# Attention: the weave of the log-sum-exps, the place of the forget-gate rows, of the factors and of four copies

## The chip, the cores and the metric

The kernel runs on one core of one Trainium2 chip. The metric is the device time of one execution in microseconds (us). A core has a matrix engine (TensorE, PE in the profile, its weight loads PEld), VectorE (DVE), ScalarE (ACT), GpSimd (POOL) and SyncE (SP); SP issues nearly all DMAs here, one after the other. Each engine works through its own queue in order.

## The reference

A decoder trunk of two layers over 528 tokens (16 learned ones ahead of 512), width 1024: forgetting attention, a gated MLP with a short convolution, a gated linear recurrence, and another such MLP. All is float32. The change lies in the attention of layer 0, with 16 heads of 64:

```python
xn = rms_norm(h, norm_g)
q, k, v, f_logit, o_gate = jnp.split(xn @ w_in, [D, 2 * D, 3 * D, 3 * D + H], axis=-1)
q = rms_norm(q.reshape(B, L, H, hd), q_gain).astype(jnp.float32) * (hd ** -0.5)
k = rms_norm(k.reshape(B, L, H, hd), k_gain).astype(jnp.float32)
log_f = jax.nn.log_sigmoid((f_logit + b_f).astype(jnp.float32))
c = jnp.cumsum(log_f, axis=1).transpose(0, 2, 1)
...
s = jnp.einsum('bqhd,bkhd->bhqk', q_blk, k)
s = s + c_blk[..., None] - c[:, :, None, :]
s = jnp.where(q_pos[:, None] >= key_pos[None, :], s, -jnp.inf)
p = jax.nn.softmax(s, axis=-1)
...
o = o * jax.nn.sigmoid(o_gate)
return o @ w_out
```

## The kernel before

Activations lie with features on the partitions and the 528 tokens along the free axis. A float32 matrix product is made of three matmuls on split operands: each operand is a rounded part `hi` (float32r) and a remainder `lo`, and hi·hi, lo·hi and hi·lo are accumulated (L263, L266, L267 in `proj_unit`; L312 in `values`). `weights` loads a weight tile to `raw` (L207, issued by SP, two buffers), casts it to `hi` on ScalarE (L210) and subtracts to get `lo` on VectorE (L126, the line of the helper `sub`).

The attention (`fox`) takes its 16 heads as eight pairs. A loop over p from -3 to 7 makes one step of the pipeline. In each step generators are woven by `weave`: every part has a number, and at each turn the part whose yielded sum over that number is smallest is advanced to its next yield. Thus a number larger than the sum of the part's yields makes it end before the step does. The parts of step p are:

- the fill: the projections of query and key of pair p+3 (`stage_a`), of values for two pairs at a time (`stage_v`, by `values`), of the output gate (`stage_g`, from step 4), and in the last step half of the output projection for four blocks (`stage_p`);
- `stage_n(p + 2)`: the factors of the query and key norm. `stage_a` ends with sums of squares (`strow`, L548), which go by four small DMAs to `am` (L553), through a reciprocal root on VectorE, and by two DMAs to `rows` (L563). `stage_n` spreads them by a matmul (L577, PSUM bank d, one buffer), multiplies query and key by them on VectorE (L578), splits into hi and lo (`stg`), and calls `pack`;
- `pack`: six DMAs (L604) that put the split query and key of two heads into two of six slots `pk` (`k1`, `q1`, `k2`, `q2`);
- `stage_l(p + 1)`: first four small DMAs (L613) that put the cumulated forget gates `cneg` into two rows of each head's `k1`, then `lse` for each of the two heads: scores by block of queries (L735, L736, the mask L738, PSUM bank s with four buffers), the row maximum on VectorE (L748, L754, L755), the sum of exponentials on ScalarE (L119), the logarithm, a transpose by matmul of `lr` (L770), and three DMAs of `lrow` into two rows of `q1` (L775, L776). Its yields add up to 2.0 a head;
- `stage_t(p)`: after a yield of 2.75 the attention proper (`attend`): scores with the log-sum-exp already in the operands (L792, L793), masked on VectorE (L796), the exponential on ScalarE (`pt`), times values (L807, PSUM bank c).

Values come in blocks of 128 tokens and one of 16 (the "lone" ones). The 16 are computed in another way (L295, L302), and `put` copies each block from PSUM (bank p, two buffers) to `v`, times the token's norm factor: L593, on ScalarE.

The program's order gives each instruction its priority; at build time a scheduler with a model of durations puts them into the queue of each engine, so that an instruction may be placed ahead of an earlier one that is not ready yet by that model. On the chip the queues run in the order so fixed.

Of the kernel before, what the change touches and what calls it, by code (L numbers as in the profile page):

```python
# [16 lines left out]
AF = mybir.ActivationFunctionType  # L17
ALU = mybir.AluOpType
# [9 lines left out]
NPAIR = 8  # L28
# [28 lines left out]
def weave(*parts):  # L57

    live = [[g, 0.0, cost] for g, cost in parts if g is not None]
    while live:  # L60
        x = min(live, key=lambda r: r[1] / r[2])
        try:
            x[1] += next(x[0])
        except StopIteration:
            live.remove(x)


def take(gen, share):

    for cost in gen:  # L70
        yield cost
        share -= cost
        if share <= 0:
            return
# [8 lines left out]
class Builder:  # L83
# [297 lines left out]
    def fox(self, ctx):  # L381
        nc, tc, a = self.nc, self.tc, self.a
# [53 lines left out]
        for g in range(4):  # L436
            t0, tn = full[g % 2]
# [10 lines left out]
        def stage_f():  # L448

            zr = s2.tile([HF, T], F32, name="zr", tag="strow", bufs=1)  # L450
            for t0, tn in full:
                psf = self.bank("c")
                o = psf[:HF, :tn]
                for k in range(KT):
                    xh, xl = self.xhi[:, k, t0 : t0 + tn], self.xlo[:, k, t0 : t0 + tn]
                    mm(psf[:, :tn], wfs[k][:, 0:P], xh, start=k == 0, stop=False)
                    mm(psf[:, :tn], wfs[k][:, 32 : 32 + P], xl, start=False, stop=k == KT - 1)
                    if k % 2:
                        yield 0.44
                zv = zr[:, t0 : t0 + tn]  # L460
                nc.scalar.copy(zv, psf[32 : 32 + HF, :tn])
                nc.vector.tensor_tensor(zv, o, zv, ALU.add)
                nc.vector.tensor_tensor(zv, zv, self.rsb[:HF, t0 : t0 + tn], ALU.mult)
            nc.sync.dma_start(z, zr.rearrange("h (j c) -> h j c", c=CW))
# [28 lines left out]
        def stage_g(ms, outs):  # L493

            for m, out in zip(ms, outs):
                wt = self.weights(a["wg"][m], KT)
                for t0, tn in full:
                    ps = bank()
                    yield from self.proj_unit(ps[:, :tn], [wt], self.x, t0, tn)
                    nc.vector.tensor_tensor(out[:, t0 : t0 + tn], ps[:, :tn], self.rsb[:, t0 : t0 + tn], ALU.mult)  # L500


                e = self.sqp.tile([P, T], F32, name="e", tag="sq")
                nc.vector.tensor_scalar(out, out, -87.0, None, ALU.max)
                self.act(e, out, AF.Exp, scale=-1.0)
                self.act(out, e, AF.Ln, bias=ones1)
                self.act(out, out, AF.Exp, scale=-1.0)
                nc.vector.scalar_tensor_tensor(e, e, 1.0, out, ALU.add, ALU.mult)
                nc.vector.scalar_tensor_tensor(out, e, 2.0, out, ALU.subtract, ALU.mult)
# [58 lines left out]

        def stage_n(p):

            raw, rows = scaled.pop(p)
            stg = s2.tile([P, 4, T], F32R, name="stg", tag="stg", bufs=1)
            for w_, nm in ((0, "q"), (1, "k")):
                hh, ll = stg[:, 2 - 2 * w_, :], stg[:, 3 - 2 * w_, :]
                for i, (t0, tn) in enumerate(full):
                    bc = self.bank("d")
                    mm(bc[:, :tn], selr[:, 2 * w_ + i, :], rows, start=True, stop=True)  # L577
                    nc.vector.tensor_tensor(  # L578
                        raw[nm][:, t0 : t0 + tn], raw[nm][:, t0 : t0 + tn], bc[:, :tn], ALU.mult
                    )  # L580
                    yield 0.11
                nc.scalar.copy(hh, raw[nm])
                self.sub(ll, raw[nm], hh.bitcast(F32))
            pack(p, stg)

        def stage_v(p):

            v = vs[(p // 2) % NV]

            def put(t, o):  # L590
                tn = o.shape[0]
                r = rs[:tn, rcol[t] : rcol[t] + 1]
                nc.scalar.activation(v[:tn, t, :, :], o.rearrange("p (b c) -> p b c", c=64), AF.Copy, scale=r)  # L593

            yield from self.values(a["wv"][p // 2], KTL, put, lone, 16, "ppppp")

        def pack(p, stg):
            packs[p] = []
            for hd in range(2):
                head = 2 * p + hd  # L600
                d = slots[head % NSLOT]
                packs[p].append(d)
                sl = slice(64 * hd, 64 * hd + 64)
                dma = lambda o, i: nc.sync.dma_start(o.bitcast(F32), i.bitcast(F32))  # L604
                dma(d["pk"][0:64, 0:2, :], stg[sl, 0:3:2, :])
                dma(d["pk"][0:64, 2:4, :], stg[sl, 0:4:3, :])
                dma(d["pk"][64:128, 2:4, :], stg[sl, 1:3, :])

        def stage_l(p):
            for hd, d in enumerate(packs[p]):  # L610
                head = 2 * p + hd
                for x in range(2):
                    nc.sync.dma_start(  # L613
                        d["k1"][64 + x : 65 + x, :].rearrange("x (j c) -> x j c", c=CW).bitcast(F32),
                        cneg[8 * head : 8 * head + 8, x, :].bitcast(F32),
                    )
            for d in packs[p]:
                yield from self.lse(d, s2, identb, maskq)

        def stage_t(p):  # L620

            yield 2.75
            for o0, o1 in ((0, 256), (256, 528)):
                po = self.bank("c")
                yield from self.attend(o0, o1, p, packs[p], vs[(p // 2) % NV], po, s2, maskk)
                nc.vector.tensor_copy(gate[:, p, o0:o1], po[:, : o1 - o0])
# [38 lines left out]
        def stage_p():  # L665

            for m in range(NEARLY):
                nc.sync.dma_start(self.h[:, m, :], a["h0"][:, m, :])
                yield from out_proj(m, 0, 4, hold=True)
# [6 lines left out]
        for p in range(-3, NPAIR):  # L676
            fill, cost = [], 0.0
            if p % 2 and 0 <= p + 1 < NPAIR:
                fill.append(vgen[p + 1])
                cost += half if p > 0 else 2 * half  # L680
            if p + 3 < NPAIR:
                fill.append(stage_a(p + 3))
                cost += 12.8
            if p % 2 == 0 and 0 <= p < NPAIR - 2:
                fill.append(take(vgen[p + 2], half))
                cost += half
            if p in gplan:
                fill.append(stage_g(gplan[p], [late[m % 4] for m in gplan[p]]))
                cost += 5.4 * len(gplan[p])
            if p == NPAIR - 1:  # L690
                fill.append(stage_p())
                cost += 2.7 * NEARLY
            weave(
                (chain(*fill), 0.97 * cost),
                (stage_n(p + 2) if 0 <= p + 2 < NPAIR else None, 1.0),
                (stage_l(p + 1) if 0 <= p + 1 < NPAIR else None, 4.3),
                (stage_t(p) if p >= 0 else None, 8.5),
                (stage_f() if p == -2 else None, 3.5),
            )
            if p == -2:  # L700
                forget()
            gated += gplan.get(p, ())
            while gated and p >= max(gated[0], 5 + gated[0] // 4):
                m = gated.pop(0)
                o = gate[:, m, :]
                nc.vector.scalar_tensor_tensor(o, o, -1.0, late[m % 4], ALU.mult, ALU.mult)
                ohi, olo = (slots[s]["pk"][:, m % 4, :] for s in ((4, 5) if m < 4 else (0, 1)))
                nc.scalar.copy(ohi, o)
                self.sub(olo, o, ohi.bitcast(F32))
                ox.append((ohi, olo))  # L710
# [832 lines left out]
```

## Time and profile before

| | us |
|---|---|
| median of 3 runs | 1457.14 |
| lowest and highest of them | 1457.02, 1458.89 |
| the profiled execution | 1460.8 |
| its span, first to last instruction | 1458.7 |

Mean granted TensorE clock over the span: 0.994. In the profile a line such as `L793 MATMUL pss<-pk` names the line of the kernel, the operation, and the tiles written and read; `pss` is PSUM bank s. A bracket at the end of a timeline row is the engine's idle time before the instruction and what ended it. Matmuls overlap: where they follow each other without a stop, the distance of their starts, and not the duration, tells their pace. Queue rows of SP are the time that issuing took, not the transfer. Times in the trace count from the first instruction. The attention lies between the start and about 370 us; step -1 begins near 45 us, the pair-by-pair attention (`stage_t`) runs from 100 to 355 us.

### The profile page before, as it was taken

The numbers are of one execution on the slowest core, as the hardware profiler recorded it, in microseconds if no ns is written. First come the engines' busy times: TensorE is split into PE (matmuls) and PEld (weight loads), VectorE is DVE, ScalarE is ACT, GpSimd is POOL, SyncE is SP. The second block draws the span as 40 slices with busy tenths as digits, with TensorE's granted clock in tenths as the row PEclk, the third lists the DMA queues.
The fourth block names the chain that finished last, engine by engine and source line by source line (L and its number), as shares of the span: only waits on it lengthen the run. The fifth ranks groups of instructions, "written<-read, shape, count | busy, mean of one in ns | idle before, by whom it ended". The sixth has DMA issues, their size and how long they took to land.

```text
span 1458.7 us, 29188 instructions
## 1 busy us (share of the span) xinstructions
PE 1431.1 (98%) x11482; PEld 1351.5 (93%) x11482; DVE 973.4 (67%) x2080; ACT 664.6 (46%) x1293; POOL 151.5 (10%) x271
## 2 busy tenths in 40 slices
PE   7999999998999999999999999999999999999998
PEld 6888888888999999999998999999999999999997
DVE  7555555774667665666785676677667877866773
ACT  5355555573434444333563223332445565544551
POOL 7000000001112100111001101011011110000000
PEclk9999999999999999999999999999999999999999
DMA  4443344435999884678737527284587795544542
GB/s 160 119 106 90 90 107 125 134 82 128 299 231 242 214 253 138 171 193 199 217 93 181 147 43 178 68 188 110 124 235 162 213 280 166 174 141 138 162 145 88
DMA packets 99697, 230.98 MB, mean 158 GB/s; under 512 B 13528, under 2 KB 15320, under 8 KB 99560
## 3 DMA queue, kind: packets, MB, share of 16 engines
q1 hardware_dynamic: 79400, 188.47, 40.5%
q0 software_dynamic: 20160, 40.64, 18.3%
q8 instruction: 90, 1.47, 0.4%
q14 instruction: 47, 0.39, 0.1%
HBM read 213.62 MB, written 75.24 MB: 198 GB/s over the span
## 4 chain that ended last, share of the span: by engine, by line
PE 90%; DMA 4%; DVE 2%; ACT 2%; issue 1%; SPq 1%; ACTq 0%; DVEq 0%
PE psp L263 8%; PE psp L267 8%; PE psp L266 8%; PE pss L263 8%; PE pss L267 8%; PE pss L266 8%; PE psp L312 6%; PE psp L1300 2%; PE psp L1301 2%; PE psp L1302 2%; PE psc L807 2%; PE pss L961 1%; PE psp L1194 1%; PE psp L1195 1%; PE psp L1196 1%; PE psd L1302 1%
## 5 line engine op out<-in xcount | busy, mean ns | idle before, releaser
L210 ACT CAST hi<-raw 128x1024 fp32r<-128x1024 f32 (+3 forms) x250 | 234.2, 940 | 365.4 <-PE psp L266 88.7
L126 DVE TENSOR_TENSOR lo<-raw,hi 128x1024 fp32r<-128x1024 f32 (+3 forms) x254 | 275.5, 1088 | 98.4 <-ACT hi L210 94.6
L263 PE MATMUL psp<-xhi,hi 128*128 128x264 f32 (+1 forms) x984 | 283.2, 289 | 6.3 <-ACT xhi L332 6.3
L266 PE MATMUL psp<-xlo,hi 128*128 128x264 f32 (+1 forms) x984 | 283.4, 288 | 2.6 <-DVE xlo L333 2.6
L267 PE MATMUL psp<-xhi,lo 128*128 128x264 f32 (+1 forms) x984 | 284.3, 289 | 0.0
L263 PEld LDWEIGHTS psp<-xhi,hi 128*128 128x128 f32 x984 | 186.6, 190 | 9.6 <-ACT xhi L332 6.3
L266 PEld LDWEIGHTS psp<-xlo,hi 128*128 128x128 f32 x984 | 187.1, 190 | 4.9 <-DVE xlo L333 3.5
L267 PEld LDWEIGHTS psp<-xhi,lo 128*128 128x128 f32 x984 | 187.1, 190 | 1.5 <-issue 1.5
L267 PE MATMUL pss<-xhi,lo 128*128 128x264 f32 (+3 forms) x520 | 149.9, 288 | 0.0
L263 PE MATMUL pss<-xhi,hi 128*128 128x264 f32 (+3 forms) x520 | 149.3, 288 | 0.1
L266 PE MATMUL pss<-xlo,hi 128*128 128x264 f32 (+3 forms) x520 | 149.2, 287 | 0.0
L232 POOL DMA_DIRECT2D s<-gu x80 | 66.2, 846 | 332.6 <-DMA s<-gu 297.0
L263 PEld LDWEIGHTS pss<-xhi,hi 128*128 128x128 f32 x520 | 97.8, 188 | 0.9 <-ACT xhi L332 0.3
L267 PEld LDWEIGHTS pss<-xhi,lo 128*128 128x128 f32 x520 | 97.7, 188 | 0.7
L266 PEld LDWEIGHTS pss<-xlo,hi 128*128 128x128 f32 x520 | 97.8, 188 | 0.7
L312 PE MATMUL psp<-hi,xhi 128*128 128x256 f32 x232 | 67.6, 291 | 3.0 <-ACT v L593 3.0
L267 PE MATMUL pss<-room,lo 128*128 128x512 f32 (+1 forms) x182 | 70.3, 386 | 0.0
L266 PE MATMUL pss<-room,hi 128*128 128x512 f32 (+1 forms) x182 | 70.2, 386 | 0.0
L263 PE MATMUL pss<-room,hi 128*128 128x512 f32 (+1 forms) x182 | 69.4, 386 | 0.6 <-ACT hi L210 0.6
L1167 ACT CAST hi<-left 128x768 fp32r<-128x768 f32 (+1 forms) x56 | 43.3, 781 | 54.2 <-PE psp L1195 18.0
L1302 PE MATMUL psp<-xhi,lo 128*128 128x258 f32 x240 | 67.7, 282 | 0.0
L1300 PE MATMUL psp<-xhi,hi 128*128 128x258 f32 x240 | 67.7, 282 | 0.0
(488 smaller groups left out, 3811.3 us busy)
## 6 DMA issues: line engine op xcount, KB each, us to landing
raw<-gu SPq DMA_DIRECT2D x48, 512.0 KB
s<-gu SPq DMA_DIRECT2D x80, 256.0 KB
s<-gu POOLq DMA_DIRECT2D x80, 256.0 KB, 5.7
raw<-gu SPq DMA_DIRECT2D x60, 256.0 KB
pk<-stg SPq DMA_DIRECT2D x48, 264.0 KB
raw<-s SPq DMA_DIRECT2D x40, 256.0 KB
raw<-s SPq DMA_DIRECT2D x20, 512.0 KB
raw<-wqk SPq DMA_DIRECT2D x14, 512.0 KB
```

What stands on the lines that cost most here:

```text
L126: self.nc.vector.tensor_tensor(out, x, y, ALU.subtract)
L210: nc.scalar.copy(hi, raw)
L232: nc.gpsimd.dma_start(out, y, accum_op=ALU.add, max_dma_last_dim=4 * n)
L263: ins = mm(ps, hi[:, i, :], xh, start=k == 0, stop=False)
L266: mm(ps, hi[:, i, :], xl, start=False, stop=False)
L267: mm(ps, lo[:, i, :], xh, start=False, stop=k == total - 1)
L312: mm(ps[:tn, :256], y[:, t0 : t0 + tn], w, start=n == 0, stop=n == 23)
L807: ins = mm(o, v[:, j, 2 * (p % 2) + hd, :], w[hd][0], start=j == 0, stop=j == last)
L1167: nc.scalar.copy(hi, raw)
L1300: mm(ps, hi[:, k0 + k, :], xh, start=start and k == 0, stop=False, skip_group_check=not start)
L1301: mm(ps, hi[:, k0 + k, :], xl, start=False, stop=False, skip_group_check=not start)
L1302: mm(ps, lo[:, k0 + k, :], xh, start=False, stop=k == 3, skip_group_check=not start)
```

## The change

Four edits, all in `fox`:

1. `stage_l` is woven with 5.7 instead of 4.3, `stage_n` with 1.3 instead of 1.0.
2. `stage_n` begins with a yield of 0.45, so that its first matmul comes later in the step.
3. The four DMAs of the forget-gate rows are taken out of `stage_l` into `decays`, which for the pairs 1 to 7 is called right behind `pack`; for pair 0, where the gates are not there yet at that time, it stays at the start of `stage_l`.
4. The copy of the 16 lone values in `stage_v` is done by VectorE; the blocks of 128 stay on ScalarE.

```diff
         def stage_n(p):
 
+            yield 0.45
             raw, rows = scaled.pop(p)
...
             def put(t, o):
                 tn = o.shape[0]
                 r = rs[:tn, rcol[t] : rcol[t] + 1]
-                nc.scalar.activation(v[:tn, t, :, :], o.rearrange("p (b c) -> p b c", c=64), AF.Copy, scale=r)
+                o = o.rearrange("p (b c) -> p b c", c=64)
+                if tn == 16:
+                    nc.vector.tensor_scalar(v[:tn, t, :, :], o, r, None, ALU.mult)
+                else:
+                    nc.scalar.activation(v[:tn, t, :, :], o, AF.Copy, scale=r)
...
                 dma(d["pk"][64:128, 2:4, :], stg[sl, 1:3, :])
-
-        def stage_l(p):
+            if p:
+                decays(p)
+
+        def decays(p):
+
             for hd, d in enumerate(packs[p]):
                 head = 2 * p + hd
                 for x in range(2):
...
+        def stage_l(p):
+            if p == 0:
+                decays(0)
             for d in packs[p]:
                 yield from self.lse(d, s2, identb, maskq)
...
-                (stage_n(p + 2) if 0 <= p + 2 < NPAIR else None, 1.0),
-                (stage_l(p + 1) if 0 <= p + 1 < NPAIR else None, 4.3),
+                (stage_n(p + 2) if 0 <= p + 2 < NPAIR else None, 1.3),
+                (stage_l(p + 1) if 0 <= p + 1 < NPAIR else None, 5.7),
```

## The prediction, made before the result was known

> **What bounds the kernel now.** I read the page first, then the waits of TensorE alone within the attention stage (the first 420 us), then the timelines round each of its long waits.
>
> ```profile
> span 1458.7 us, 29188 instructions
> PE 1431.1 (98%) x11482; PEld 1351.5 (93%) x11482; DVE 973.4 (67%) x2080; ACT 664.6 (46%) x1293; POOL 151.5 (10%) x271
> PE 90%; DMA 4%; DVE 2%; ACT 2%; issue 1%; SPq 1%; ACTq 0%; DVEq 0%
> ```
>
> The reader is to see that TensorE (PE) is the bound: busy 98% of the span, and 90% of the chain that ended last. The change removes no matmul and adds none. It can win only where PE stands still or runs at a lower clock, and lose only by making it stand still in new places. So the question is which of PE's waits in the attention stage the edits reach. The waits of PE, columns total, times, longest:
>
> ```profile
> PE psp L263 <- ACT xhi L332: 6.3, 1, 6.3
> PE pss L792 <- DMA pk<-lrow: 4.0, 1, 4.0
> PE psp L312 <- ACT v L593: 3.0, 3, 1.7
> PE pss L735 <- DMA pk<-cneg: 1.0, 1, 1.0
> PE psd L577 <- DMA rows<-yr: 1.0, 1, 1.0
> PE pss L770 <- DVE lr L126: 0.8, 1, 0.8
> ```
>
> The first is the start of the kernel, which the diff leaves alone. The other five add up to 9.8 us and are, line by line, what the diff touches: the log-sum-exp rows (lrow, lr), the values (v), the forget-gate rows (cneg) and the factors (rows). A wait of PE also costs clock, which the windows show (PE busy and instructions, then the same of the other engines, PEclk, DMA):
>
> ```profile
> 50.00:57.00 7.00, 5.35 (x32) 5.21 (x32) 3.97 (x10) 2.79 (x6) 0.00 (x0) 0.76 0.27 86
> 305.00:333.00 28.00, 26.62 (x203) 23.19 (x202) 19.58 (x58) 17.74 (x54) 0.95 (x1) 1.00 0.27 69
> 337.00:343.00 6.00, 5.73 (x27) 5.74 (x28) 2.02 (x5) 1.56 (x4) 1.46 (x2) 0.52 0.46 68
> 343.00:355.00 12.00, 12.00 (x100) 10.13 (x98) 4.76 (x13) 5.25 (x13) 0.98 (x2) 1.00 0.74 176
> ```
>
> The granted clock is 0.52 in the 6 us behind the wait for lrow and 1.00 again from 343 us.
>
> **Part 1: log-sum-exps at 5.7 instead of 4.3 (stage_l).** The weave takes, at each turn, the part with the smallest share done, share being the sum of its yields over its number. One pair's stage_l yields 2 x (4 x 0.3 + 0.6 + 0.2) = 4.0. It ended at 4.0/4.3 = 0.93 of a step and now ends at 4.0/5.7 = 0.70. In the steps p = 0 to 5 nothing waits for its end, as stage_t of that pair starts only 2.75/8.5 = 0.32 into the next step. The last step is different, because few projections are left to run in front of stage_t(7). PE's timeline and the queue of SP there:
>
> ```profile
> 332.72 0.22 PE L770 MATMUL pss<-identr,lr 128*128 128x128 f32 x1
> 332.95 0.28 PE L793 MATMUL pss<-pk 128*128 128x256 f32 x1
> 337.27 0.58 PE L792 MATMUL pss<-pk 98*128 98x256 f32 x1 [4.03 <-DMA pk<-lrow]
> 338.08 0.42 PE L266 MATMUL psp<-pk,hi 128*128 128x264 f32 x1
> 338.30 0.42 PE L267 MATMUL psp<-pk,lo 128*128 128x264 f32 x1
> 343.34 0.28 PE L266 MATMUL psp<-pk,hi 128*128 128x264 f32 x1
> 343.46 0.28 PE L267 MATMUL psp<-pk,lo 128*128 128x264 f32 x1
> 333.60 1.26 SPq L775 DMA_DIRECT2D pk<-lrow  x2
> 334.90 0.61 SPq L776 DMA_DIRECT2D pk<-lrow  x1
> ```
>
> The transpose of the last log-sum-exps (L770) runs at 332.72, its row is sent until 334.90 + 0.61 = 335.51, and it is there at 337.27, 1.8 us on. PE had asked at 333.2 and sat 4.03 us. Step p = 6 lasts about 28 us (305 to 333). Ending 0.93 - 0.70 = 0.23 of it earlier moves L770 by 6.4 us, and the landing to 337.3 - 6.4 = 330.9, ahead of 332.95. So the 4.03 us go. With them goes the slow clock: from 337.3 to 342.7 the matmuls start 0.22 us apart (338.08, 338.30), later 0.12 (343.34, 343.46), so 5.4 us of work would have taken 5.4 x 0.52 = 2.8 us, and 2.6 us are won. Sum of part 1: **-6.6 us**. Late next is VectorE: the same step already shows PE held 0.8 us by lr, and the max, subtract and exp work of two heads now stands closer together. I take 0 for that wait; its bounds are -0.8 (gone) and +1.6 (once per head).
>
> [...]
>
> **Part 2: the factors later (stage_n).** Four broadcasts stood at 0, 0.11, 0.22 and 0.33 of a step and the packing at 0.44. They now stand at 0.45/1.3 = 0.35 to 0.60, and the packing at 0.89/1.3 = 0.68. The middle steps take some 34 us (130 to 164), so the first moves by 12 us, the packing by 8.2.
>
> ```profile
> 139.51 0.28 PE L266 MATMUL psp<-xlo,hi 128*128 128x264 f32 x1
> 140.77 0.36 PE L577 MATMUL psd<-rows,selr 128*128 128x264 f32 x1 [0.97 <-DMA rows<-yr]
> 57.69 6.14 SPq L604 DMA_DIRECT2D pk<-stg  x6
> 193.58 2.82 SPq L613 DMA_DIRECT2D pk<-cneg  x4
> 73.02 0.25 PE L735 MATMUL pss<-pk 66*128 66x16 f32 x1 [1.03 <-DMA pk<-cneg]
> ```
>
> The wait for rows at 139.51 is covered by the 12 us: **-1.0 us**. What the delay uses up is the time between packing and the next step's log-sum-exps, now 0.32 x 34 = 10.9 us.
>
> **Part 3: the forget-gate rows with the packing (decays).** No DMA is added; for pairs 1 to 7 the four of L613 go from the start of stage_l to behind the six of L604. SP then issues 6.14 + 2.82 = 9.0 us on end, and the last lands 1.8 us later (as lrow did): 10.8 us, against 10.9 available. Before, they were issued in the step itself and landed 2.8 + 1.8 = 4.6 us into it. So the log-sum-exps can begin up to 4.7 us sooner, and that is also what a late packing may lose before they are worse off. The rows wait for cneg (done before step p = -1) and for the slot's last reader, stage_t of three pairs before: both done. Behind the ten stand the square sums (am), the factors (rows) and weight loads; two weight buffers cover them. Pair 0 keeps its place, so the 1.03 us at 73.02 stays. Value: **+1.0 us**, one further wait of that kind; bounds 0 and, at seven of them, +7.
>
> **Part 4: the lone values by VectorE (put).** Four instructions (the groups by shape of ScalarE; the source view of L299 for the nearest of VectorE):
>
> ```profile
> L593 ACT ACTIVATE v<-psp,rst 16x256 f32<-16x256 f32 x4 | 1.8, 456 | 0.9 <-PE psc L807 0.9
> L299 DVE COPY part<-psp x4: 405/408/424, 46.6 to 226.1; 128x256 f32<-128x256 f32 x4
> ```
>
> By VectorE each should take 408 to 456 ns, 1.7 us in all on an engine that is 67% busy: nothing by itself, and at most 1.7 if no gap took it. What counts is where they queue:
>
> ```profile
> 100.98 0.28 PE L312 MATMUL psp<-hi,xlo 128*128 128x256 f32 x1
> 102.42 0.39 PE L312 MATMUL psp<-hi,xhi 128*128 128x256 f32 x1 [1.17 <-ACT v L593]
> 100.96 1.05 ACT L210 CAST hi<-raw 128x1024 fp32r<-128x1024 f32 x1 [1.30 <-DMA raw<-wqk]
> 101.91 0.46 ACT L593 ACTIVATE v<-psp,rst 16x256 f32<-16x256 f32 x1
> 98.46 0.19 DVE L556 TENSOR_TENSOR am<-am,et 64x33 f32<-64x33 f32 x1 [2.21 <-DMA am<-strow]
> 102.04 1.23 DVE L126 TENSOR_TENSOR lo<-raw,hi 128x1024 fp32r<-128x1024 f32 x1 [0.70 <-ACT hi L210]
> 49.66 1.05 ACT L210 CAST hi<-raw 128x1024 fp32r<-128x1024 f32 x1 [3.94 <-DMA raw<-wqk]
> 51.26 0.82 ACT L593 ACTIVATE v<-psp,rst 128x256 f32<-128x256 f32 x2
> 51.79 0.39 PE L312 MATMUL psp<-hi,xhi 128*128 128x256 f32 x1 [1.65 <-ACT v L593]
> ```
>
> At 100.98 PE waits for the PSUM bank of the lone value, whose copy stands on ScalarE behind a weight cast that itself waits for a load. VectorE is at work on other things from 98.46 and idle 0.70 us before 102.04, so it would free the bank earlier: **-1.2 us**. At 51.79 it is different: of the two copies the one of the ordinary block comes first (51.26), PE starts again 0.53 us after that, and that copy stays on ScalarE behind the same cast. So those 1.65 us and the 1.7 of clock I leave in: 0, with -3.4 as the bound.
>
> **Sum.** -6.6 - 1.0 + 1.0 - 1.2 = -7.8 us. Against the profiled execution (1460.8 us, of which 1458.7 are the span) this gives 1453.0; the median of the runs shown is 1457.1, 3.7 us less, and from it the forecast is 1457.1 - 7.8 = **1449.3**. The stage after it is PE-bound too (PE busy 12.00 of 12 from 343), so that what is won at 337 us should last to the end.
>
> **Rivals.**
> 1. *The last row comes as late as before.* The lr of L770 could be set by VectorE and ScalarE, not by the weave; the 0.8 us at lr speaks for it, PE busy 26.62 of 28 with VectorE only 19.58 of 28 speaks against. Then -1.0 + 1.0 - 1.2 = -1.2: 1455.9.
> 2. *Slower: the weights behind the packing.* Ten DMAs are sent in one block, and the packing waits for stg with all loads behind it on SP. If a weight cast then comes late, PE stops as at 51.79: 1.65 + 1.7 = 3.4 us a time. For it speaks that both waits for v go back to a cast that waited for raw<-wqk (3.94 and 1.30 idle); against, that no projection waits for a cast anywhere in the list of PE's waits. It decides from 3 of the six steps on (10.2 against the 8.8 gained); at four, 13.6 - 8.8 = +4.8: 1461.9.
> 3. *More goes.* With the VectorE copy the values' banks change hands otherwise and the 3.4 us at 50 us go as well, and the 0.8 at lr: -12.0, 1445.1.
>
> **How the numbers follow.** Forecast 0.53, with a range of its own of 1446 to 1454 (parts 1 and 4 at their bounds); rival 1 0.20; rival 2 0.17; rival 3 0.10. A measurement of this kernel tells about 0.2% (2.9 us) from no change. The forecast and rival 3 are faster by more, with a little of rival 1: 0.64; the rest of rival 1 is the same, 0.19; rival 2 slower, 0.17. The range from 1444 to 1461 holds everything but the far half of rival 2 and the tails.
>
> **What would show it.** Part 1: no wait for lrow at L792 and a clock of 1.00 through the last step. Part 2: no wait at L577. Part 3: L613 behind L604 on SP; at most one wait at L735. Part 4: no wait for v at the second group of values, the first unchanged. Wrong would be: a wait of PE over 1.5 us within steps 0 to 5 with a clock under 1.00, above all L263 or L312 for hi or lo.

## The result and the profile after

The change makes the kernel slower: 1471.78 us (median; 1466.72 to 1475.41) against 1458.02 (1456.31 to 1460.94) for the kernel before on the same chip, a ratio of 1.0087 with an interval of 1.0061 to 1.0113. The forecast was 1449.3 in a range of 1444 to 1461: wrong in sign. The profiled execution of the changed kernel took 1466.76 us and is among its shortest, so the trace shows less of the loss than the median does.

The page of the changed kernel, the same three lines as before (the transpose L770 is now L782, the scores L792 are L804, the log-sum-exp scores L735 are L747):

```profile
span 1464.7 us, 29178 instructions
PE 1430.6 (98%) x11482; PEld 1351.1 (92%) x11482; DVE 975.6 (67%) x2084; ACT 662.0 (45%) x1289; POOL 152.0 (10%) x271
PE 90%; DMA 4%; DVE 2%; ACT 2%; issue 1%; SPq 0%; ACTq 0%; DVEq 0%
```

The same matmuls, the same bound, and PE busy for 0.5 us less than before (1431.1) in a span 6.0 us longer: the time went into waits. Up to the end of the last product with the values PE runs 2607 matmuls in both kernels. It ends them at 355.1 us before, having been busy for 335.75 us, and at 365.0 us after, busy for 336.52: it stood still for 9.1 us more. PE's waits in the first 420 us (total, times, longest):

```profile
PE pss L782 <- DVE lr L126: 6.5, 2, 5.5
PE psp L263 <- ACT xhi L332: 6.2, 1, 6.2
PE psp L312 <- ACT v L598: 4.6, 3, 2.2
...
PE pss L747 <- ACT pt L119: 2.2, 1, 2.2
PE psp L263 <- ACT rawq L540: 1.6, 1, 1.6
PE pss L804 <- DVE lrow L784: 1.4, 1, 1.4
PE psd L578 <- DMA rows<-yr: 1.2, 2, 0.7
```

The wait for the DMA of lrow (4.0) and the one for cneg (1.0) are gone. In their place the wait for lr has grown from 0.8 to 6.5 us, and three are new: for pt, for rawq and for lrow on VectorE. Where the work was lost is told by windows, first of the kernel before, then of the changed one (stretch, length, busy time and count of PE, PEld, DVE, ACT and POOL, granted clock, DMA share, GB/s):

```profile
100.00:164.00 64.00, 61.86 (x494) 53.51 (x493) 34.87 (x119) 34.90 (x109) 0.90 (x8) 1.00 0.36 94
222.00:240.00 18.00, 17.78 (x139) 14.25 (x139) 9.52 (x37) 7.34 (x24) 0.23 (x2) 1.00 0.38 109
307.00:370.00 63.00, 57.59 (x433) 52.05 (x432) 37.55 (x97) 31.77 (x82) 5.82 (x7) 0.95 0.51 126
```

```profile
100.00:164.00 64.00, 59.29 (x470) 50.86 (x469) 35.57 (x120) 35.93 (x108) 0.67 (x6) 1.00 0.43 118
222.00:240.00 18.00, 14.43 (x60) 9.93 (x59) 8.34 (x33) 7.53 (x25) 0.20 (x2) 0.62 0.27 90
307.00:370.00 63.00, 56.28 (x417) 48.56 (x417) 35.36 (x99) 31.40 (x91) 4.46 (x7) 0.92 0.42 107
```

The matmuls (the count behind PE's busy time) fall short in three places: by 24, by 79 and by 16. In the 18 us from 222 both the waits and the clock of 0.62 are new. What follows the last product with the values takes 1104 and 1100 us, and 1100 to 1108 in every other profile of this study, in no order that goes with the edits. So the loss arises in the attention.

The end of step p = 6, where before all was quiet, on PE and then on SP:

```profile
324.64 0.23 PE L750 MATMUL pss<-maskq,identb 128*128 128x128 bf16 x1
330.36 0.45 PE L782 MATMUL pss<-identr,lr 128*128 128x128 f32 x1 [5.49 <-DVE lr L126]
330.60 0.54 PE L804 MATMUL pss<-pk 98*128 98x256 f32 x1
```

```profile
316.66 0.63 SPq L788 DMA_DIRECT2D pk<-lrow  x1
```

PE stands 5.49 us at the transpose of the last pair's first head. Behind it in its queue stands a score of pair 6 (L804), whose log-sum-exp row had been sent by 317.3 us. In the queue that score is held back by the transpose ahead of it. How the transpose came to stand there is the question of the experiments.

### The profile page after: what moved, and what is told of

Read it like the earlier page. It is cut to its first block, busy times and chain, and to the rows that moved or that the text cites. A ratio compares the mean times of both kernels' runs of the same rounds, so it can differ in the third digit from the quotient of the medians.

```text
span 1464.7 us, 29178 instructions
## 1 busy us (share of the span) xinstructions
PE 1430.6 (98%) x11482; PEld 1351.1 (92%) x11482; DVE 975.6 (67%) x2084; ACT 662.0 (45%) x1289; POOL 152.0 (10%) x271
## 4 chain that ended last, share of the span: by engine, by line
PE 90%; DMA 4%; DVE 2%; ACT 2%; issue 1%; SPq 0%; ACTq 0%; DVEq 0%
PE psp L263 9%; PE psp L267 9%; PE psp L266 9%; PE pss L267 8%; PE pss L266 8%; PE pss L263 8%; PE psp L312 5%; PE psp L1314 2%; PE psp L1312 2%; PE psp L1313 2%; DMA raw<-gu 2%; PE psc L819 2%; PE psp L1206 1%; PE psp L1207 1%; PE psp L1208 1%; PE pss L973 1%
```

## The experiments

All ratios are to the kernel before on the same chip, with 95% intervals.

| run | what it is | ratio | interval |
|---|---|---|---|
| e1_late | only the factors later | 0.9976 | 0.9962 to 0.9990 |
| e2_lse | only 5.7 | 1.0051 | 1.0034 to 1.0069 |
| e3_rows | only the rows with the packing | 0.9998 | 0.9981 to 1.0016 |
| e4_lone | only the lone copies by VectorE | 1.0013 | 0.9998 to 1.0028 |
| e9_lse56 | only 5.6 | 1.0093 | 1.0073 to 1.0112 |
| e10_lse555 | only 5.55 | 1.0006 | 0.9991 to 1.0021 |
| e6_lse55 | only 5.5 | 0.9952 | 0.9937 to 0.9968 |
| e11_lse_t26 | 5.7, first yield of `stage_t` 2.6 | 0.9946 | 0.9932 to 0.9961 |
| e5_lse_t19 | 5.7, first yield of `stage_t` 1.9 | 1.0029 | 1.0009 to 1.0049 |
| e7_after_t19 | whole change, first yield 1.9 | 1.0056 | 1.0039 to 1.0074 |
| e8_no_lse | whole change with 4.3 | 1.0019 | 0.9997 to 1.0041 |
| e12_after55 | whole change with 5.5 | 1.0044 | 1.0027 to 1.0060 |
| e13_late55 | 5.5 and the factors later | 0.9965 | 0.9950 to 0.9979 |
| e14_lone55 | 5.5 and the lone copies | 1.0039 | 1.0018 to 1.0060 |
| e15_no_lone | whole change without the lone copies | 1.0108 | 1.0080 to 1.0136 |
| e16_no_late | whole change without the later factors | 1.0140 | 1.0122 to 1.0159 |
| e17_after_gp | whole change, rows issued by GpSimd | 1.0041 | 1.0021 to 1.0062 |
| e18_lse_rows | 5.7 and the rows with the packing | 1.0074 | 1.0049 to 1.0100 |

**Each edit alone.** Four kernels, each with one part of the diff: the factors, then the number of `stage_l`, the rows, and the lone copies (the last two as in the diff above).

```diff
         def stage_n(p):
+            yield 0.45
...
-                (stage_n(p + 2) if 0 <= p + 2 < NPAIR else None, 1.0),
+                (stage_n(p + 2) if 0 <= p + 2 < NPAIR else None, 1.3),
```

> Only the factors later (the yield of 0.45 and 1.3 instead of 1.0 for stage_n). Theory 1 (queue of SP): the packing, the sums and the loads behind it on SP come later, so weight casts on ScalarE wait for late loads, and PE stops for what stands behind the cast; this edit alone then costs most of the 12 us: ratio 1.005 to 1.010, with the log-sum-exps of the pairs 2 to 7 starting 5 us or more later than before. Theory 2 (proportion): the 5.7 is the cause, and this edit alone gives 0.999 to 1.002. Theory 3 (forget-gate rows behind the packing): also 0.999 to 1.002 here.

```diff
-                (stage_l(p + 1) if 0 <= p + 1 < NPAIR else None, 4.3),
+                (stage_l(p + 1) if 0 <= p + 1 < NPAIR else None, 5.7),
```

> Only 5.7 instead of 4.3 for stage_l. Theory 1: it does no harm by itself; the wait of 4 us for lrow in the last step goes, ratio 0.995 to 0.999. Theory 2: log-sum-exps and scores crowd VectorE and ScalarE, new waits of PE for lr or for the exponentials, ratio 1.005 to 1.010. Theory 3: as theory 1.

```diff
...
+            if p:
+                decays(p)
...
+        def stage_l(p):
+            if p == 0:
+                decays(0)
```

> Only the forget-gate rows sent with the packing. Theories 1 and 2: within 0.2% of before, since SP sent these rows ahead of the packing in the kernel before as well, when their slot came free. Theory 3: ratio 1.004 or more, with a packing or a load that stands behind the rows.

```diff
...
+                if tn == 16:
+                    nc.vector.tensor_scalar(v[:tn, t, :, :], o, r, None, ALU.mult)
...
```

> Only the copy of the lone values by VectorE. All theories: 0.998 to 1.001; the wait of 1.2 us for v at the second group of values is gone or smaller.

The largest single loss is in the edit from which the largest gain was forecast: 5.7 alone costs 0.5%. The factors alone gain 0.24% (some 3.5 us), though the wait for rows that they were to remove is still there (1.2 us in e1_late). The rows alone do nothing. The lone copies alone do nothing that is clear of zero. Of the theories, that of proportion expected the size of the loss of 5.7 (1.005 to 1.010); none expected a gain from the factors.

**Where the weave turns.** The first theory after e2 was a matter of order. A head's `lse` yields 4 x 0.3 + 0.6 = 1.8, then issues its tail with the transpose, and only then the last 0.2. `stage_t` begins, after its yield of 2.75 over a number of 8.5, at a share of 0.3235. With 4.3 the first head has reached 1.8/4.3 = 0.419 before its tail, so scores of the pair at work are issued ahead of the transpose. With 5.7 it is at 1.8/5.7 = 0.316, the smaller share, and the transpose of the next pair's first head is issued ahead of every score. Behind it in PE's queue the scores wait, as L804 did behind the 5.49 us above. The first score of the second pair and that transpose, of the kernel before, the changed one, and e2_lse:

```profile
134.55 0.29 PE L792 MATMUL pss<-pk 98*128 98x256 f32 x1
144.28 0.22 PE L770 MATMUL pss<-identr,lr 128*128 128x128 f32 x1
```

```profile
148.46 0.33 PE L782 MATMUL pss<-identr,lr 128*128 128x128 f32 x1
148.63 0.33 PE L804 MATMUL pss<-pk 98*128 98x256 f32 x1
```

```profile
147.78 0.22 PE L770 MATMUL pss<-identr,lr 128*128 128x128 f32 x1
147.83 0.33 PE L792 MATMUL pss<-pk 98*128 98x256 f32 x1
```

Before, the score runs 9.7 us ahead of the transpose; with 5.7 right behind it, 13 to 14 us later than before. The rival theory was crowding: that log-sum-exps closer together simply overload VectorE and ScalarE, more so the larger the number. Four kernels were to separate them, the first two with 5.7 or the whole change and a smaller first yield of `stage_t`:

```diff
         def stage_t(p):
...
-            yield 2.75
+            yield 1.9
```

> 5.7 for stage_l as in the run with that edit alone (ratio 1.0051 there), but stage_t begins with a yield of 1.9 instead of 2.75, so that its first four scores stand on PE ahead of the transpose of the next pair's first head again, as in the kernel before. Theory A (order): 5.7 does harm only since it puts the first score behind that transpose, whose chain takes some 12 us; here the scores of a pair begin before the transpose, the waits for lr in the last two steps go, and the ratio is 0.995 to 1.000. Theory B (crowding): the log-sum-exps stand as close together as in the run with 5.7 alone, and the ratio stays at 1.004 to 1.008.

> The whole change, with stage_t beginning at 1.9 instead of 2.75. Theory A: most of the loss (ratio 1.0087) goes, 0.996 to 1.002. Theory B: 1.006 or more.

```diff
-                (stage_l(p + 1) if 0 <= p + 1 < NPAIR else None, 4.3),
+                (stage_l(p + 1) if 0 <= p + 1 < NPAIR else None, 5.5),
```

> Only 5.5 for stage_l, 4% less than 5.7. 1.8/5.5 = 0.327 lies above 2.75/8.5 = 0.324, where 1.8/5.7 = 0.316 lies below, so one score of each pair is ahead of the transpose and the others behind. Theory A: ratio between 1.000 and 1.004, the first score some 10 us earlier. Theory B: as with 5.7, 1.004 to 1.006.

In the fourth the number stays at 4.3 and the other three edits are made:

> The whole change but the log-sum-exps at 4.3 as before. Both theories: the loss goes, 0.996 to 1.001 (factors later 0.9976, rows 0.9998 and lone values 1.0013 alone add up to 0.9987). If it stays above 1.004, the three other edits do harm together that none does alone.

At 5.5 (1.8/5.5 = 0.327, one score ahead of the transpose) the sign turns: 0.9952, a gain that neither theory expected. The 1.9 brings four scores ahead again, as before, and wins back less than half of what was lost, 1.0029 and 1.0056; both miss what theory A expected (0.995 to 1.000, 0.996 to 1.002). By the order at this turn alone they should have done better. With 4.3 and the other three edits the ratio is 1.0019, a little above the 0.996 to 1.001 that both theories expected. So the edge itself was tried next: 5.6 (0.3214, still under 0.3235), 5.55 (0.3243, just over), and 5.7 with a yield of 2.6 (2.6/8.5 = 0.306, under 0.316), beside the whole change with 5.5.

```diff
         def stage_t(p):
...
-            yield 2.75
+            yield 2.6
...
-                (stage_l(p + 1) if 0 <= p + 1 < NPAIR else None, 4.3),
+                (stage_l(p + 1) if 0 <= p + 1 < NPAIR else None, 5.7),
```

> Only 5.6 for stage_l. 1.8/5.6 = 0.3214 lies just below the 2.75/8.5 = 0.3235 at which stage_t takes its first score, so the transpose of the next pair's first head stands ahead of all scores, as with 5.7. Theory A (order): as slow as 5.7, ratio 1.003 to 1.007. Theory B (crowding, smooth in the number): between 5.5 (0.9952) and 5.7 (1.0051), 0.998 to 1.002.

> Only 5.55 for stage_l, one per cent below the run before it. 1.8/5.55 = 0.3243 lies just above 0.3235: one score ahead of the transpose, as with 5.5. Theory A: 0.994 to 0.998. Theory B: within 0.2% of the run with 5.6.

> 5.7 for stage_l with the yield at the start of stage_t 2.6 instead of 2.75: 2.6/8.5 = 0.306 lies below 1.8/5.7 = 0.316, so one score stands ahead of the transpose again while the log-sum-exps stand as close together as in the change. Theory A: 0.994 to 0.999, and projections are left for the last steps (50 or more when the last pair's log-sum-exps begin, none with 5.7 alone). Theory B: 1.004 to 1.007, as 5.7 alone.

> The whole change with 5.5 instead of 5.7. Theory A: the whole change loses 0.9% by that order alone, 0.994 to 1.000. Theory B: 1.005 to 1.009.

In e9_lse56 the transpose starts at 146.73 us and the first score at 146.78, as in e2_lse. In e11_lse_t26 the score is ahead again:

```profile
133.59 0.28 PE L792 MATMUL pss<-pk 98*128 98x256 f32 x1
140.63 0.22 PE L770 MATMUL pss<-identr,lr 128*128 128x128 f32 x1
```

For 5.7 alone this decides for the order and against crowding. e2_lse and e11_lse_t26 have the same 5.7 and differ in one yield, 2.75 or 2.6: 1.0051 and 0.9946. Between 5.55 and 5.6, a change of one per cent, lie 0.9%. And e6_lse55 and e11_lse_t26, with different numbers, have traces in which the order of PE's 11482 matmuls differs in four of them, and the same time within 0.4 us (1452.40, 1452.08). The number acts through the queue order that it makes and not by itself. In the traces of all seven kernels with the yield of 2.75 and a number of 5.6 or 5.7 no score of any pair stands ahead of the next pair's first transpose, and all seven are at 1.0041 or above.

The order at this turn is not the whole of it, though. 5.55 has it as 5.5 has and is 0.5% slower (expected by theory A 0.994 to 0.998, measured 1.0006), and some 400 of its 11482 matmuls stand elsewhere than in e11_lse_t26. The whole change with 5.5 has one score ahead for each pair, and still loses 0.44%: theory A expected 0.994 to 1.000, theory B 1.005 to 1.009, and neither holds. About half of the loss of the whole change went with the order, the other half did not. Why 5.6 is slower than 5.7 was not shown either; in e9_lse56 the stop at 222 us, treated below, comes on top.

What happens at the end is seen in the projections (those that read xhi) left for the last pair, from the start of its log-sum-exps to the end of the attention; windows of that tile alone, of the kernel before, the changed one, e2_lse, e11_lse_t26 and e12_after55:

```profile
307.50:355.00 47.50, 6.72 (x35) 5.23 (x33) 0.00 (x0) 0.00 (x0) 0.93 0.42 95
```

```profile
319.90:365.00 45.10, 1.93 (x11) 1.43 (x9) 0.00 (x0) 0.00 (x0) 0.89 0.44 108
```

```profile
316.90:362.00 45.10, 0.00 (x0) 0.00 (x0) 0.00 (x0) 0.00 (x0) 0.85 0.42 108
```

```profile
301.70:349.00 47.30, 9.11 (x44) 7.07 (x43) 0.00 (x0) 0.00 (x0) 0.96 0.45 113
```

```profile
318.50:363.60 45.10, 0.14 (x1) 0.00 (x0) 0.00 (x0) 0.00 (x0) 0.89 0.44 110
```

Where the scores stand behind the transpose, other products have run ahead of both, and these are then missing at the end: 35 are left before, 11 and 0 with the transpose first, 44 in e11_lse_t26 (expected were 50 or more there, and none with 5.7 alone). With little or nothing left to run, PE stands at lr (5.49 us above) and its clock over these windows is 0.89 and 0.85.

This count also tells where the order at the turn does not. In e12_after55 only 1 is left although a score stands ahead, in e5_lse_t19 0 and in e7_after_t19 1, although four do, and in e10_lse555 7: PE stands at lr for 5.2, 2.9, 2.9 and 4.1 us in them, and none is faster than before. The three kernels with a gain over 0.3% (e6_lse55, e11_lse_t26, e13_late55) have 44 left. So the transpose ahead of the scores is one way to use the projections up early, and not the only one. It is a pattern over the traces and not an experiment, and it has exceptions: e9_lse56 has 19 left and is slower than e2_lse, and e4_lone has 53 and gains nothing.

In e11_lse_t26 PE's waits behind the start of the kernel are these:

```profile
PE psp L312 <- ACT v L593: 2.2, 2, 1.5
PE pss L770 <- DVE lr L126: 1.1, 1, 1.1
PE pss L735 <- DMA pk<-cneg: 1.0, 1, 1.0
PE pss L792 <- DVE lrow L772: 0.8, 1, 0.8
```

The 4.0 us for the DMA of lrow are gone here too, and lr costs 1.1. This kernel, with 5.7 alone and the one yield, is faster than the kernel before and the changed one: 1452.08 us.

**The 79 matmuls at 222 us.** The second loss looked like the forecast's second rival, weights late behind the packing. The changed kernel, SP, then ScalarE, then PE:

```profile
210.46 6.10 SPq L609 DMA_DIRECT2D pk<-stg  x6
216.62 2.95 SPq L621 DMA_DIRECT2D pk<-cneg  x3
219.67 2.69 SPq L553 DMA_DIRECT2D am<-strow  x4
222.46 1.03 SPq L207 DMA_DIRECT2D raw<-wg  x2
```

```profile
226.10 1.04 ACT L210 CAST hi<-raw 128x1024 fp32r<-128x1024 f32 x1 [6.02 <-DMA raw<-wg]
227.05 0.38 ACT L119 ACTIVATE pt<-pss 128x256 f32<-128x256 f32 x1
```

```profile
224.86 0.33 PE L804 MATMUL pss<-pk 98*128 98x128 f32 x1 [1.39 <-DVE lrow L784]
227.48 0.49 PE L747 MATMUL pss<-pk 66*128 66x144 f32 x1 [2.18 <-ACT pt L119]
```

SP issues for 12 us without a pause before it comes to the weights of the output gate (wg). ScalarE has the cast of those weights at the head of its queue and stands 6.02 us, with the exponential (pt) behind it. PE needs the bank that this exponential reads and stands 2.18 us for it. The same load in the kernel before, SP and ScalarE:

```profile
214.51 6.06 SPq L604 DMA_DIRECT2D pk<-stg  x6
220.67 3.62 SPq L553 DMA_DIRECT2D am<-strow  x4
224.41 1.81 SPq L207 DMA_DIRECT2D raw<-wg  x2
```

```profile
227.68 0.29 ACT L119 ACTIVATE pt<-pss 128x144 f32<-128x144 f32 x1
228.03 1.06 ACT L210 CAST hi<-raw 128x1024 fp32r<-128x1024 f32 x1
```

The load is issued even later, at 224.41, and costs nothing: the cast stands behind exponentials whose data are there. So it is not the place on SP alone, but where the cast stands among the exponentials. e9_lse56 shows it again: the rows are not moved there, and its cast of wg waits 7.56 us at the same place. To part the two, the rows of the whole change were issued by GpSimd, and the rows were added to 5.7 alone:

```diff
-                    nc.sync.dma_start(
+                    nc.gpsimd.dma_start(
```

> The whole change with the forget-gate rows issued by GpSimd, so that they no longer stand on SP ahead of the sums and the weight loads. If the queue of SP makes the further loss: 1.003 to 1.006, and ScalarE waits less than 3 us for raw<-wg before 300 us. If not: 1.007 to 1.010.

> 5.7 and the forget-gate rows with the packing; factors and lone values as before. If the rows on SP make the further loss: 1.008 or more. If not: as 5.7 alone, 1.003 to 1.007.

Without the rows on SP the whole change gives 1.0041 in place of 1.0087, and ScalarE's waits for weights between 100 and 300 us change as follows, first the changed kernel, then e17_after_gp:

```profile
ACT hi L210 <- DMA raw<-wg: 8.1, 2, 6.0
ACT hi L210 <- DMA raw<-wqk: 2.7, 2, 1.9
```

```profile
ACT hi L210 <- DMA raw<-wqk: 13.1, 4, 5.1
ACT hi L210 <- DMA raw<-wg: 0.3, 1, 0.3
```

The wait for wg goes, others come for wqk. Both the ratio and this wait are as expected if the queue of SP makes the further loss. But e18_lse_rows, with the rows behind the packing, waits 2.0 us for wg, and e2_lse without them 2.1, so the rows by themselves don't make the long wait; and e18_lse_rows is at 1.0074 against 1.0051 with overlapping intervals, e3_rows at 0.9998. A cost of the rows on SP within the whole change is possible, but it isn't shown by itself.

**Do the other edits add up?** One kernel each with 5.5, which is good alone, and with one part of the whole change taken out:

> 5.5 for stage_l and the factors later; rows and lone values as before. If the gains add up: 0.993 (0.9952 x 0.9976). If the late factors hurt beside early log-sum-exps, since packing then comes in the way of the next pair's start: 1.000 or more.

> 5.5 for stage_l and the lone values by VectorE. If they add up: 0.9965. If the copy on VectorE changes the order at the start so that attention begins later (first score near 105 us instead of 100): 1.000 or more.

> The whole change without the lone values by VectorE (5.7, late factors, rows). If the lone copies cost the further 0.4%: 1.003 to 1.006, as 5.7 alone or less. If the late factors do: 1.007 or more.

> The whole change without the late factors (5.7, rows, lone values). If the late factors cost the further 0.4%: 1.004 to 1.006. If the lone copies do: 1.007 or more.

They don't. The factors change nothing beside 5.5 (0.9965 against 0.9952) and help the whole change by half a per cent (1.0140 without them). The lone copies turn 0.9952 into 1.0039 beside 5.5, yet the whole change without them is no faster (1.0108). So neither of the two parts was found to make the further 0.4%. The four single ratios multiply to 1.0038, the whole change has 1.0087. What the lone copies do is seen in e4_lone, in PE's waits:

```profile
PE psp L263 <- ACT rawq L540: 1.6, 1, 1.6
PE psp L312 <- ACT v L597: 1.5, 2, 1.3
```

The waits for v fall from 3.0 to 1.5 us as forecast, but the queues are laid out anew: the first log-sum-exp score comes at 77.1 us instead of 73.0, a wait of PE for a copy (rawq) ends at 73.5 us, and the first attention score moves from 100.3 to 105.6. It does so wherever the lone copies are on VectorE and a score stands ahead of the transpose: 104.5 to 106.5 us in e4_lone, e7_after_t19, e8_no_lse, e12_after55 and e14_lone55, whose ratios are 1.0013 to 1.0056, against 98.4 to 100.4 in the others with a score ahead. Why the change of an engine for four copies moves the order so far stays open, as does why the edits don't add.

## Why the prediction was wrong

**Part 1, the step that failed.** It said that in the steps p = 0 to 5 "nothing waits for its end", and that ending 0.23 of a step earlier "moves L770 by 6.4 us". The weave's number doesn't move an instruction in time. It moves it in PE's queue, and here what stood behind it waited for its operands (5.49 us for lr at the transpose in step 6). The row for pair p+1 was read as an event that only the next step needs; in the queue the scores of pair p stood behind it. The last transpose went from 332.7 to 341.8 us instead of to 326.3. The wait for lrow did go, as forecast, and lr took its place: forecast at 0 with bounds of -0.8 and +1.6, measured +5.7. What the failed step cost is shown for 5.7 alone: 1.0051 with the transpose first, 0.9946 with one score ahead of it. For the whole change it is about half (1.0087, and 1.0044 with 5.5); where the rest comes from stays open. With one score ahead, e11_lse_t26 gains 0.54% and e6_lse55 0.48%, 7.9 and 7.0 us of 1459, near the forecast of 6.6. That nearness is partly luck: e10_lse555 has the same order and gains nothing, and in e11_lse_t26 the half clock at 52.6 us, which the forecast left in, is gone too (granted clock over the first 100 us: 0.98, before 0.97). The shares 0.316 and 0.3235 could both have been worked out beforehand from the numbers of the kernel.

**Part 2.** The wait for rows didn't go (1.0 to 1.2 us); the edit is worth -3.5 us alone and nothing beside 5.5, so its gain comes from elsewhere than the -1.0 forecast.

**Part 3.** The value of +1.0 is within the interval of e3_rows. The premise "Before, they were issued in the step itself" was wrong: counted through at four rows and six packing DMAs a pair, the trace of before has the rows of every pair from 1 to 7 sent ahead of the packing of that pair. The edit thus sends them later, not sooner, and the log-sum-exps could not begin 4.7 us sooner by it. The first row and the packing of pair 3:

```profile
131.58 0.69 SPq L613 DMA_DIRECT2D pk<-cneg  x1
...
150.41 6.15 SPq L604 DMA_DIRECT2D pk<-stg  x6
```

**Part 4.** The waits for v fell by 1.5 us in e4_lone (forecast 1.2), and rose to 4.6 us in the whole change. The copies took 462 to 472 ns on VectorE, little more than the 408 to 456 forecast; what failed is "nothing by itself", since the edit also changed the order of the queues. Alone it gives +1.9 us by the ratio, with zero within the interval.

**The rivals.** The second rival had the sign right and one of the chains: the cast of wg waits for its load, and PE stops. Its rule (a stop for three of the six steps, 3.4 us each: 1.65 us of waiting and the 1.7 us of clock that part 4 counts too, an estimate of 7.0 us x (1 - 0.76) from the window at 50 us) was not what decided, since the order of the transpose gives a loss with no row moved (e2_lse, e9_lse56). The first rival, that the last row comes as late as before, was near in its cause, the lr of VectorE, and had no loss in it. The new waits at lr were the thing listed as "late next" and priced at 0. The sign of being wrong, a wait over 1.5 us within steps 0 to 5 at a clock under 1.00, came too, though for pt (2.18 us) and not for hi or lo.

## What to carry to other kernels

When parts are woven by shares, work out at which share each part issues what others stand behind, and compare these shares before and after: here 0.316 against 0.3235 or 0.306 made the difference of one per cent between two kernels alike but for one yield. In these traces an instruction that waited held up what stood behind it in its queue (5.49 us at the transpose, with a score behind it whose row had been sent by 317.3 us; 6.02 us at the cast, with an exponential behind it), and independent work that had run early was missing at the end (11 and 0 projections left in place of 35), where the stall then showed, far from its cause. So count also how much of that work is left for the last stage. A schedule edit should be measured with neighbouring numbers and beside the other edits: single results neither carried over to the next number nor added up.

## What the runs showed of the hardware

From 222 to 240 us of the changed kernel PE was busy for 14.43 of 18 us and no wait was longer than 2.18 us, yet the granted clock was 0.62; the trace's clock records put it at half speed from 225.3 us for 13.7 us. PE's windows before, and during, the half speed:

```profile
221.90:225.30 3.40, 2.01 (x14) 1.56 (x13) 1.61 (x11) 0.00 (x0) 0.00 (x0) 1.00 0.49 154
225.30:239.00 13.70, 11.52 (x42) 7.92 (x42) 6.05 (x20) 7.27 (x24) 0.10 (x1) 0.50 0.23 80
```

The two rows are stretch, length and busy times as above, the clock third from the end. PE was idle for 1.4 of the 3.4 us before, and during the half speed it was busy for 11.52 of 13.7 us. Between 40 us and the end of the attention the stretches at half speed lasted 3.4 and 6.8 us in the kernel before, 3.4, 13.7 and 10.2 in the changed one, and 3.4 in e11_lse_t26 (a clock of 0.88 over the 14 us from 324). They add up to 10.2, 27.3 and 3.4 us. In the kernel before, at the wait for lrow, the clock fell at 335.9 us, 2.7 us after PE had begun to wait at 333.2. How much of a loss is the clock behind the waits was not separated: up to the end of the attention PE stood still for 9.1 us more in the changed kernel and was busy for only 0.8 us more.
